# GpSimd adds for the conv LayerNorm sums, half of the first merge moved earlier, and a quartered load, in a hybrid recurrence/convolution block on eight Trainium2 cores

## The chip, the cores and the metric

The kernel runs on the eight cores of one Trainium2 chip, one batch row of 4096 tokens on each core; the cores do not talk to each other. The metric is the device time of one execution, taken on the slowest core, in microseconds (us). Cores 0 to 3 are die 0, cores 4 to 7 are die 1.

Some executions, of every kernel here, fall into a slower state: one die, at times both, shows a lower granted TensorE clock (0.81 to 0.97, where an undisturbed die shows 0.98 to 0.99) and the time is 1 to 20 per cent longer. Only fast runs are compared. On some chips one die was disturbed in most runs; there I also use the *undisturbed-die mean*: the median of a die's four cores, averaged over all runs, slow ones too, and all dies whose median clock was at least 0.98. It leaves out the slowest core and so is about 12 us shorter than the time, but it is compared only with the same figure of the kernel before on the same chip.

Five engines run in parallel, each in its own strict order: TensorE (PE in the profile), VectorE (DVE), ScalarE (ACT), GpSimd (POOL) and SyncE (SP, which issues most DMA transfers here).

## The reference, cut to what matters

```python
proj = h @ w_in            # q, f, i, o-gate | glu value, glu gate | merge gate A, merge gate B
# mixer A: HGRN2 gated recurrence (chunks of 64), then rms_norm, gate, and
y_a = o @ w_hg_out
# mixer B: GLU -> causal depthwise conv of 31 taps -> LayerNorm -> silu -> pointwise
u   = glu_v * sigmoid(glu_g)
u   = causal_depthwise_conv(u, conv_w, conv_b)
u   = silu(layer_norm(u, conv_ln_g, conv_ln_b))     # "conv LN": mean and variance over 1024 channels
y_b = u @ w_conv_out
mixed = sigmoid(gate_a) * y_a + sigmoid(gate_b) * y_b            # "merge"
h = layer_norm(alpha * h + mixed @ w_out)                        # "outproj"
h = layer_norm(alpha * h + (silu(g) * u_) @ w_ffn_out)           # "ffn1", "ffn2"
```

Shapes: 4096 tokens a core, width 1024, feed-forward width 2816.

## The kernel before

The program is recorded first and then list-scheduled: every operation gets an engine, a modelled duration and a place in that engine's queue, and the place is fixed when the kernel is built. What an engine finds at its head and cannot start yet blocks all that stands behind it (one such wait of 8.0 us is followed through the trace below).

**Phase 1** has 32 steps (4 head pairs, 8 tiles of 512 tokens) of the recurrence. A step is a chain: it needs TensorE, then ScalarE, VectorE and GpSimd, then TensorE again. The gaps of that chain are filled with 144 units of GLU and convolution work. A conv unit is 32 small matmuls into one PSUM bank, a copy into one of two store buffers, and a DMA store of the conv output to DRAM (`ys`). `CLEAD` says how many steps before the end the conv units must all be recorded.

```python
yst = [A.at(f"y{i}", yo + i * 2048, [128, 4, 128], F32) for i in range(2)]     # two store buffers
...
def conv_unit(q, g):
    ...
    mmg(lst, ...)                                   # conv matmuls into PSUM bank ps
    ys = yst[G % 2]
    for r0, n in rows:                              # copy PSUM -> store buffer, on ACT or DVE
        cp_any(ys[r0:r0 + n, :, ::-1], ps[r0:r0 + n].rearrange("p (a b) -> p a b", a=4), scale=0.5)
    for jj, (r0, n) in enumerate(rows):             # store buffer -> DRAM
        dma("sp", dst, ys[r0:r0 + n], ..., wr=[("ys", G, jj)], nbytes=600000)
    relps("c", ps)
```

**Phase 2** goes over eight tiles: conv LN (`conv_ln`), merge (256 matmuls, eight weight blocks of 1 MB), outproj (64), transposes of h (`h_trans`), ffn1 (352) and ffn2 (176). In conv LN, TensorE adds over the channels by multiplying with a matrix of ones, 16 matmuls a tile:

```python
def conv_ln(pool="a"):
    pS1, pS2 = newps(pool), newps(pool)
    for j in range(8):                              # 8 blocks of 128 channels
        ts_(b1[:], cpre[:, j, :], cb[:, j:j + 1], None, ALU.add, ALU.bypass)     # DVE: y + bias, to bf16
        act(b2[:], cpre[:, j, :], AF.Square, bias=cb[:, j:j + 1])                # ACT: its square
        mmg([(pS1, ones1024[:], b1[:], j == 0, j == 7)])
        mmg([(pS2, ones1024[:], b2[:], j == 0, j == 7)])
        yield
    ...                                             # mean, 1/std, then 8 x (DVE, DVE, ACT) -> un
```

The **transition** from phase 1 to phase 2 is a queue of work recorded behind the last conv unit:

```python
def tail():
    load_cpre(0)                                    # 2 MB of conv output, needs the last conv store
    loads(0)
    yield from conv_ln("c")
    load_cpre(1)
    yield from merge(0, ...)
```

Steady state of phase 2, tile i: outproj(i) and ffn2(i-1), `h_trans(i)`, merge(i+1), then ffn1(i) with conv LN of tile i+2 spread under it.

## Time and profile before

Time before: 2432.92 us, median of three runs (2431.75 to 2434.59).

The page of the profiled execution, kernel before, first its line of busy time (us, share of the span, instructions), then the shares of the chain of waits that ended last:

```profile
PE 2321.6 (96%) x14400; PEld 1145.9 (47%) x14400; DVE 1349.1 (56%) x1917; ACT 1002.6 (41%) x1391; POOL 114.2 (5%) x287
...
PE 90%; DMA 3%; DVE 2%; ACT 2%; issue 2%; SPq 0%; POOL 0%; DVEq 0%; ACTq 0%; POOLq 0%
```

TensorE is the bound. So a change can win only where it takes work from TensorE or removes time in which TensorE waits or runs below full clock. The windows of the slowest core (core 5) say where such time lies. Columns: stretch in us, its length, busy time and instructions of each engine, granted TensorE clock, DMA share and GB/s.

```profile
core 5: us, PE busy (x) PEld busy (x) DVE busy (x) ACT busy (x) POOL busy (x), PEclk, DMA share, GB/s
60.00:740.00 680.00, 671.43 (x5928) 378.29 (x5925) 503.73 (x686) 449.16 (x574) 92.70 (x233) 0.99 0.80 137
740.00:860.00 120.00, 98.84 (x1142) 59.61 (x1142) 74.67 (x116) 77.86 (x93) 13.85 (x34) 0.95 0.82 208
860.00:945.00 85.00, 69.75 (x319) 30.99 (x316) 40.19 (x66) 29.99 (x43) 0.59 (x1) 0.88 0.51 164
945.00:1025.00 80.00, 76.98 (x375) 34.97 (x376) 57.41 (x90) 38.78 (x58) 0.53 (x1) 1.00 0.66 229
```

Phase 1 up to 740 us leaves TensorE idle for 9 us of 680. From 740 to 1025 us it is idle for 39 of 285 us, and its clock falls. The largest waits of TensorE (for what, us in total, times, longest), first of 60 to 740 us, then of 740 to 1025 us:

```profile
PE pst L442 <- DVE sb_y_18_60 L497: 5.9, 1, 5.9
```
```profile
PE pst L442 <- ACT sb_q_64_106 L469: 11.6, 2, 10.6
PE pst L454 <- DVE sb_K_28_70 L478: 7.7, 2, 4.8
```

The largest gap ends at 885.42 us: after its first eight matmuls merge 0 waits until conv LN 0 has given back scratch tiles. The timeline shows it, and that the eight matmuls after the gap took 3.57 us, where eight of the same shape take 1.89 us in the steady part:

```profile
885.42 3.57 PE L442 MATMUL pst<-sb_xT_55,sb_W_8_50 128*128 128x512 bf16 x8 [10.57 <-ACT sb_q_64_106 L469]
```

For the rest of the text I use three marks on the TensorE timeline, means over cores 0, 1, 2, 3 and 5: **conv** (the last conv unit starts), **mix** (the first outproj matmul of tile 0), **H0** (the first h-transposes of tile 0). Before: conv at 826.0, mix at 934.7, H0 at 1008.3 us; after H0 a tile takes 191.1 us.

### The profile page before, as it was taken

Reading aid. Unit: us, or ns where it says so; the run is one execution under the profiler, and the core shown is the slowest. Engines: PE = TensorE matmul, PEld = TensorE weight load, DVE = VectorE, ACT = ScalarE, POOL = GpSimd, SP = SyncE. Lnnn points to the kernel's source line nnn. Section 1 sums busy time; section 2 is a strip of 40 time slices with the busy share of each in tenths; the row PEclk is TensorE's granted clock in tenths of the full one; section 3 lists DMA queues with packets and bytes.
Section 4 is the critical chain, followed back from the end, with each engine's and each line's share of the span. In section 5 each row is a group of like instructions: output and inputs, shape, how many; then the busy total and the mean of one; then the engine's idle time right before and its main releaser. Section 6 shows DMA issues by size and latency. Waiting matters only on the chain.

```text
span 2430.7 us, 39791 instructions; the slowest of 8 cores (2415.1 to 2430.7 us)
## 1 busy us (share of the span) xinstructions
PE 2321.6 (96%) x14400; PEld 1145.9 (47%) x14400; DVE 1349.1 (56%) x1917; ACT 1002.6 (41%) x1391; POOL 114.2 (5%) x287
## 2 busy tenths in 40 slices
PE   5999999999998869999999999999999999999997
PEld 2555545555555534444444444444444444444443
DVE  1877767777775665546445545534634724721724
ACT  4657756766665653332242242232223323311220
POOL 0211111111110100000000000000000000000000
PEclk8999999999999989999999999999999999999999
DMA  8577996799788855653663654654654663453441
GB/s 228 82 101 113 159 148 139 142 156 149 148 150 190 223 177 202 223 186 126 235 219 136 225 191 144 244 175 169 222 189 153 207 211 146 161 213 144 147 181 70
DMA packets 115824, 414.60 MB, mean 171 GB/s; under 512 B 9248, under 2 KB 42144, under 8 KB 87456
## 3 DMA queue, kind: packets, MB, share of 16 engines
q1 hardware_dynamic: 99760, 360.31, 45.0%
q0 software_dynamic: 15872, 51.74, 16.3%
q8 instruction: 119, 1.95, 0.3%
q14 instruction: 73, 0.60, 0.1%
HBM read 421.81 MB, written 70.58 MB: 203 GB/s over the span
## 4 chain that ended last, share of the span: by engine, by line
PE 90%; DMA 3%; DVE 2%; ACT 2%; issue 2%; SPq 0%; POOL 0%; DVEq 0%; ACTq 0%; POOLq 0%
PE pst L442 89%; DMA ys<-sb_y_18_60 1%; DMA sb_stg_20_62<-xt 1%; PE pst L454 1%; DMA sb_stg_20_62<-w 1%; SPq L523 0%; ACT sb_hb_69_111 L504 0%; DVE sb_R_65_107 L478 0%; ACT L469 0%; ACT sb_F_26_68 L469 0%; ACT sb_F_27_69 L469 0%; DVE sb_q_63_105 L487 0%; ACT sb_hT_93 L499 0%; ACT sb_osq_78 L469 0%; ACT sb_og_32_74 L469 0%
## 5 line engine op out<-in xcount | busy, mean ns | idle before, releaser
L469 ACT ACT_TABLE_LOAD x136 | 174.5, 1283 | 128.9 <-DVE sb_st_74_116 L926 104.8
L442 PE MATMUL pst<-sb_W_12_54,sb_xT_55 128*128 128x512 bf16 (+1 forms) x768 | 152.7, 348 | 20.0 <-ACT sb_xT_55 L568 19.8
L442 PE MATMUL pst<-sb_xT_55,sb_W_8_50 128*128 128x512 bf16 x576 | 134.3, 387 | 16.3 <-ACT sb_q_64_106 L469 10.6
L442 PE MATMUL pst<-sb_W_9_51,sb_xT_55 128*128 128x256 bf16 (+1 forms) x768 | 120.3, 308 | 3.2 <-ACT sb_og_32_74 L469 2.0
L442 PE MATMUL pst<-sb_xT_55,sb_W_10_52 128*128 128x512 bf16 x512 | 115.3, 379 | 2.0 <-DVE sb_v_75 L495 1.0
L442 PE MATMUL pst<-sb_hT_93,sb_W_12_54 128*128 128x512 bf16 x512 | 113.4, 379 | 1.4 <-DVE sb_st_77_119 L924 1.4
L442 PE MATMUL pst<-sb_hT_93,sb_W_67_109 128*128 128x512 bf16 x512 | 114.1, 379 | 0.0
L442 PE MATMUL pst<-sb_hT_93,sb_W_10_52 128*128 128x512 bf16 x512 | 113.6, 379 | 0.0
L442 PEld LDWEIGHTS pst<-sb_W_12_54,sb_xT_55 128*128 128x128 bf16 x768 | 73.9, 98 | 79.6 <-issue 25.1
L442 PE MATMUL pst<-sb_hT_93,sb_W_8_50 128*128 128x512 bf16 x480 | 106.9, 379 | 0.2 <-ACT sb_hT_93 L499 0.2
L442 PE MATMUL pst<-sb_W_11_53,sb_xT_55 128*128 128x512 bf16 (+1 forms) x512 | 92.1, 330 | 6.2 <-DVE sb_y_18_60 L497 5.9
L442 PEld LDWEIGHTS pst<-sb_xT_55,sb_W_8_50 128*128 128x128 bf16 x576 | 56.5, 99 | 87.2 <-issue 23.4
L442 PE MATMUL pst<-sb_hT_93,sb_W_66_108 128*128 128x512 bf16 x416 | 92.4, 379 | 0.0
L442 PEld LDWEIGHTS pst<-sb_W_9_51,sb_xT_55 128*128 128x128 bf16 x768 | 73.8, 98 | 37.8 <-issue 4.3
L442 PE MATMUL pst<-sb_hT_93,sb_W_9_51 128*128 128x512 bf16 x384 | 85.3, 379 | 0.0
L478 DVE TENSOR_TENSOR sb_R_50_92<-sb_R_50_92,sb_lnt_90 128x1024 f32<-128x1024 f32 x64 | 78.4, 1225 | 7.0 <-DVE sb_R_50_92 L478 0.5
L478 DVE TENSOR_TENSOR sb_R_65_107<-sb_R_65_107,sb_lnt_90 128x1024 f32<-128x1024 f32 x64 | 78.4, 1225 | 6.7
L787 DVE TENSOR_TENSOR_SCAN sb_F_26_68<-sb_smask_49,sb_F_26_68 128x512 f32<-128x512 f32 x64 | 74.8, 1208 | 9.7 <-ACT sb_F_26_68 L469 9.6
L469 ACT ACTIVATE sb_q_63_105<-pst 128x512 f32<-128x512 f32 x53 | 31.6, 597 | 117.3 <-PE pst L442 117.2
L469 ACT ACTIVATE sb_q_64_106<-pst 128x512 f32<-128x512 f32 x54 | 32.2, 597 | 114.5 <-PE pst L442 114.2
L442 PEld LDWEIGHTS pst<-sb_hT_93,sb_W_12_54 128*128 128x128 bf16 x512 | 50.0, 98 | 61.7 <-issue 1.5
L442 PEld LDWEIGHTS pst<-sb_hT_93,sb_W_10_52 128*128 128x128 bf16 x512 | 50.1, 98 | 60.4
(283 smaller groups left out, 4293.5 us busy)
## 6 DMA issues: line engine op xcount, KB each, us to landing
sb_W_8_50<-w2b SPq DMA_DIRECT2D x34, 1024.0 KB, 5.8
sb_W_12_54<-w2b SPq DMA_DIRECT2D x34, 1024.0 KB, 6.3
sb_W_9_51<-w2b SPq DMA_DIRECT2D x34, 1024.0 KB, 5.4
sb_W_66_108<-w2b SPq DMA_DIRECT2D x34, 1024.0 KB, 5.4
sb_W_10_52<-w2b SPq DMA_DIRECT2D x32, 1024.0 KB, 6.0
sb_W_67_109<-w2b SPq DMA_DIRECT2D x32, 1024.0 KB, 6.2
w2b<-w POOLq DMA_DIRECT2D x54, 512.0 KB, 13.2
sb_T_16_58<-tabb SPq DMA_DIRECT2D x32, 632.0 KB, 9.5
```

The source lines that it names most:

```text
L442: i = e.matmul(o, lhsT=l, rhs=r, start=s0, stop=s1)
L454: i = e.transpose(o, i_, ident)
L469: P.add("act", lambda e: e.activation(out=out, in_=in_, func=func, **kw), ks(in_, scale, bias) + list(er), (ks(out) if wkeys is None else ...
L478: P.add(eng, lambda e: e.tensor_tensor(out=out, in0=in0, in1=in1, op=op), ks(in0, in1), ks(out) if wkeys is None else wkeys, dur=d)
L787: P.add("dve", lambda e, f2r=f2r: e.tensor_tensor_scan(out=f2r, data0=smask[:], data1=f2r, initial=0.0, op0=ALU.mult, op1=ALU.add), ks(F2[ ...
```

## The change

Three intents. (1) GpSimd, 5% busy, adds the eight channel blocks (and the eight blocks of squares), so that two statistic matmuls a tile are left instead of 16. (2) The conv output of tile 0 is loaded in quarters, and the conv is finished earlier (`CLEAD` 4), so that conv LN 0 starts earlier. (The loads of the later tiles become four DMAs too.) (3) Merge 0 is split around it: the half that needs no conv output (gate A, 128 matmuls) is recorded in the last four recurrence steps, the other half after conv LN 0; the eight weight blocks are loaded twice. `TBIAS`, which is added to the place of the transition's work in the scheduler's list, goes to 0.

```diff
-CLEAD = 2
+CLEAD = 4
-TBIAS = 200
+TBIAS = 0
@@ once: the sum of all bias values, per partition @@
+for a, b in ((20, 4), (44, 2), (44, 1)):
+    tt_(pp[:, 44:44 + b], pp[:, a:a + b], pp[:, a + b:a + 2 * b], ALU.add)
@@ the first GLU blocks: PSUM of the conv pool in place of the recurrence pool (cut) @@
@@ load_cpre @@
-    dma("sp", cpre[:], src, "cpre", rd=[the stores of all 64 conv units], nbytes=1750000)
+    for q in qs:                       # quarters of 512 KB, each waits for its own conv stores
+        dma("sp", cpre[:, 2 * q:2 * q + 2, :], src, f"cp{q}", rd=[stores of quarter q], nbytes=440000)
@@ conv_ln @@
-    for j in range(8):
-        ts_(b1[:], cpre[:, j, :], cb[:, j:j + 1], None, ALU.add, ALU.bypass)
-        act(b2[:], cpre[:, j, :], AF.Square, bias=cb[:, j:j + 1])
-        mmg([(pS1, ones1024[:], b1[:], j == 0, j == 7)])
-        mmg([(pS2, ones1024[:], b2[:], j == 0, j == 7)])
-        yield
+    for j in range(8):
+        act(sq[:], cpre[:, j, :], AF.Square, bias=cb[:, j:j + 1])
+        if j:
+            tt_(S1[:], cpre[:, 0, :] if j == 1 else S1[:], cpre[:, j, :], ALU.add, eng="pool")
+            tt_(S2[:], prev[:] if j == 1 else S2[:], sq[:], ALU.add, eng="pool")
+        yield
+    ts_(b1[:], S1[:], pp[:, 44:45], None, ALU.add, ALU.bypass)
+    cp(b2[:], S2[:])
+    mmg([(pS1, ones1024[:], b1[:], True, True)])
+    mmg([(pS2, ones1024[:], b2[:], True, True)])
@@ tail (shortened) @@
-    load_cpre(0); loads(0); conv_ln("c"); load_cpre(1); merge(0, ...)
+def tail_a(): loads(0); merge(0, "c", (0,))               # gate A half, from step 28 on
+def tail_b(): load_cpre(0, range(3)); (when the conv is done) load_cpre(0, (3,)); conv_ln(0); load_cpre(1)
+run(merge(0, "a", (1,)))                                  # gate B half, after both
```

## The prediction

> **What bounds it now.** TensorE. The page gives PE 96% of the 2430.7 us span, and 89% of the chain of waits is its matmul line. By windows (slowest core):
> - 60 to 740 us (phase 1): PE idle about 9 us in all.
> - 740 to 1025 us (end of phase 1, tile 0, tile 1): PE busy 245.6 of 285 us, so about 39 us idle. The granted clock falls to 0.67-0.94 in four of the windows, about 11 us more. The largest single gap is 10.6 us at 885 us: the first merge waits until conv LN of tile 0 is done; conv LN itself waits for the last conv stores and a 2 MB load of conv output (issued 846, first used 861 us).
> - after 1025 us: a steady 191.1 us per tile, with PE busy 188.4.
>
> **Removed.** 14 of 16 statistic matmuls per tile, 112 in all. A dense matmul of 512 columns costs 0.2158 us (776 in 167.49 us in the chain), so 3.02 us a tile, 24 us together. Tiles 2 to 7 sit in the full-PE regime: 6 x 3.02 = 18 us, directly on the critical path. The 6 us of tiles 0 and 1 fall in the transition.
>
> **Added.** 14 fp32 adds of 128x512 a tile on GpSimd. The trace before has no such add (its POOL TENSOR_TENSORs have 8 columns). The Trainium skill, "GPSIMD Engine Reference", section 3.1, gives 4497 ns for 2048 columns; scaled, my estimate is 1.1-1.3 us each, 15-20 us a tile. The built order puts the two statistic matmuls after nine of 22 ffn1 steps (9 x 3.45 = 31 us), and the eight adds of the first sum can run earlier, so I expect no PE wait in steady state. The same page says that GpSimd shares its SBUF interface with VectorE instructions that have two SBUF inputs; VectorE is only half busy, so some stretching is harmless. Also added: 8 MB more weight loads, since merge 0 reads each block twice.
>
> **Moved.** Conv work ends two steps earlier (PE already full: neutral). Half of merge 0 (128 matmuls, 27.6 us) fills the last four recurrence steps; each holds some 17 us of its own PE work in a chain of 22-24 us. Conv LN 0 runs under them.
>
> **Transition.** Full-speed work there is 245.6 - 11 - 6 = 229 us. I expect some 24 us left over: 2-3 us a step from PE's fixed order; GpSimd's queue, where adds for tiles 0 and 1 stand ahead of the last step's small copies; and DMA, because 5-8 MB of weights plus LN tables, x and output-projection weights are wanted in about 40 us (at most 300 GB/s was seen). So about 253 us, not 285: gain 32. Startup stays DMA-bound: no gain.
>
> **Time.** 2433 - 18 - 33 = 2382 us; 8 in 10 between 2362 and 2404. Faster by over 2%: 0.54; within 2%: 0.44; slower: 0.02.
>
> **Signs.** Right: the tile period falls from 191.1 to about 188.1 us; PE count 14288; GpSimd adds near 1.2 us with PE never waiting for them in phase 2; the 10.6 us gap gone; PE idle between 740 us and the end of merge 1 near 20 us. Wrong: PE waiting on the converted sums (tiles b), i.e. adds over 2 us; PE waiting on weight tiles or the tile-1 x load; E/r copies late behind adds, so K transposes wait.
>
> **What would break it.** Adds much slower than estimated under VectorE contention; DMA starvation in merge 0's second half eating the gain; conv stores slowed in phase 1; or, the other way, a nearly gapless transition (2362).

## The result, and the profile after

Time after: 2424.23 us, median of four runs (2425.72, 2422.74, 2421.01 fast, 2783.92 slow; 2422.74 is the median of the fast ones); before, in the same rounds, 2433.76 us, median of four (2431.75 to 2437.04). The ratio is 0.9955, with an interval of 0.9936 to 0.9975. Ratios here are the mean time of one kernel's fast runs over that of the other's of the same rounds, so not quite the ratio of the medians that I quote. In the same setting a second time (run e11) it was 0.9944. So the kernel is about 11 us faster, where I had predicted 51 us.

The page of the profiled execution, kernel after, the same two lines:

```profile
PE 2301.2 (95%) x14288; PEld 1134.4 (47%) x14288; DVE 1338.9 (55%) x1880; ACT 1009.2 (42%) x1399; POOL 260.9 (11%) x399
...
PE 80%; DVE 7%; DMA 6%; issue 3%; ACT 2%; POOL 0%; SPq 0%; DVEq 0%; ACTq 0%; POOLq 0%
```

112 matmuls are gone and TensorE is busy 20 us less, but the span fell by 6.5 us in this pair of executions: TensorE's part of the chain of waits fell from 90 to 80%, and VectorE and DMA took its place. The windows of core 5, kernel after, same columns as before:

```profile
core 5: us, PE busy (x) PEld busy (x) DVE busy (x) ACT busy (x) POOL busy (x), PEclk, DMA share, GB/s
60.00:740.00 680.00, 654.58 (x5749) 364.57 (x5748) 489.52 (x669) 441.43 (x559) 83.01 (x226) 0.99 0.80 138
740.00:860.00 120.00, 109.52 (x1230) 65.72 (x1229) 79.77 (x119) 86.29 (x107) 30.91 (x46) 0.99 0.71 185
860.00:945.00 85.00, 70.58 (x390) 34.91 (x389) 51.87 (x77) 44.99 (x58) 22.59 (x19) 0.93 0.80 263
945.00:1025.00 80.00, 73.20 (x344) 32.84 (x342) 55.53 (x79) 31.15 (x50) 19.28 (x15) 0.99 0.72 236
```

The first row is the surprise: between 60 and 740 us, where the change was to do nothing, TensorE now idles for 25 us instead of 9 and has issued 179 matmuls fewer. The gain of 740 to 860 us (11 us more busy) is in part work that was left over. The waits of TensorE, kernel after, core 5, first of 60 to 740 us, then of 740 to 1025 us:

```profile
PE pst L447 <- DVE sb_u_15_57 L492: 10.1, 5, 8.0
PE pst L447 <- DVE sb_v_75 L500: 5.8, 2, 4.4
```
```profile
PE pst L447 <- ACT sb_part_94 L474: 6.7, 2, 4.9
PE pst L447 <- DMA sb_W_12_54<-w2b: 6.5, 2, 4.5
PE pst L447 <- DVE sb_U_41_83 L492: 2.2, 1, 2.2
PE pst L447 <- DVE sb_mixed_101 L483: 1.9, 1, 1.9
```

The 10.6 us gap is gone, as predicted; a row of shorter ones has come, on the first half of merge 0 (`part`), on weight blocks (`W <- w2b`), on the recurrence (`U`) and on the merge result. The longest wait of phase 1, 8.0 us on `sb_u`, is a GLU output that comes late. The chain of waits of core 5 tells why (start in us, duration in us, what):

```profile
315.97 0.61 ACT sb_y_19_61 L504
...
316.64 30.16 DMA ys<-sb_y_19_61
...
346.97 0.06 DVE sb_y_19_61 L502
...
347.58 1.25 DVE sb_u_15_57 L492
...
348.96 16.10 PE pst L447 x126
```

Read it from the top: ScalarE fills a store buffer; its store to DRAM takes 30.16 us (a 256 KB store lands in a median of 8.0 us here); VectorE, in its fixed order, has a conv copy into that same buffer at its head and waits for the store; behind it stands the GLU write `sb_u`, for which TensorE waits. Such a wait is not new: on the same core of the kernel before, a store at the same place (313 to 346 us) took 33.55 us, and TensorE waited 5.9 us behind it (`sb_y` above). The example shows how the wait comes about; the change made this one 2 us longer, and added others, as of 4.4 us at 555 us. I followed all engines from 60 us to H0 on five cores:

| mean of cores 0, 1, 2, 3, 5, us | before | after |
|---|---|---|
| TensorE idle, 60 to 740 | 6.7 | 20.5 |
| TensorE idle, 740 to H0 | 35.5 | 30.8 |
| lost to a lower clock, 60 to H0 | 10.1 | 12.3 |
| the rest: TensorE's own work and the shortest gaps | 896.0 | 893.8 |
| H0 | 1008.3 | 1017.4 |
| H0 to the end of TensorE's work | 1402.0 | 1388.7 |

(The rest is H0 less 60 and less the three rows above it. Idle time, here and below, leaves out gaps under some 0.15 us; with every gap counted, the four figures are 7.4, 21.6, 35.6 and 30.7. Clock loss is one less the granted clock, times TensorE's busy time, summed over windows of 20 us.) So the transition, which was to bring 32 us, is 9 us *later*; the part behind it gained 13 of 18 us.

### The profile page after: what moved, and what is told of

The parts are those of the page before. It is cut to its first block, busy times and chain, and to the rows that moved or that the text cites. A ratio compares the mean times of both kernels' runs of the same rounds, so it can differ in the third digit from the quotient of the medians.

```text
span 2424.2 us, 39922 instructions; the slowest of 8 cores (2411.4 to 2424.2 us)
## 1 busy us (share of the span) xinstructions
PE 2301.2 (95%) x14288; PEld 1134.4 (47%) x14288; DVE 1338.9 (55%) x1880; ACT 1009.2 (42%) x1399; POOL 260.9 (11%) x399
## 4 chain that ended last, share of the span: by engine, by line
PE 80%; DVE 7%; DMA 6%; issue 3%; ACT 2%; POOL 0%; SPq 0%; DVEq 0%; ACTq 0%; POOLq 0%
PE pst L447 79%; DMA ys<-sb_y_19_61 2%; DVE sb_R_70_112 L483 2%; DMA sb_stg_20_62<-xt 1%; DVE sb_R_50_92 L483 1%; DMA sb_W_12_54<-w2b 1%; DMA sb_T_16_58<-tabb 1%; PE pst L459 1%; DMA sb_stg_20_62<-w 1%; DVE sb_R_70_112 L488 1%; DVE sb_R_70_112 L492 0%; DVE sb_R_50_92 L492 0%; DVE sb_R_50_92 L488 0%; DVE sb_st_81_123 L946 0%; DVE sb_st_80_122 L946 0%
## 5 line engine op out<-in xcount | busy, mean ns | idle before, releaser
L447 PE MATMUL pst<-sb_xT_55,sb_W_8_50 128*128 128x512 bf16 x560 | 130.4, 385 | 12.3 <-ACT sb_part_94 L474 4.9
L447 PEld LDWEIGHTS pst<-sb_W_12_54,sb_xT_55 128*128 128x128 bf16 x768 | 74.5, 99 | 84.7 <-issue 30.2
L447 PEld LDWEIGHTS pst<-sb_W_9_51,sb_xT_55 128*128 128x128 bf16 x768 | 73.7, 98 | 40.1 <-issue 5.4
L447 PEld LDWEIGHTS pst<-sb_xT_55,sb_W_8_50 128*128 128x128 bf16 x560 | 54.8, 99 | 80.5 <-issue 18.5
L474 ACT ACTIVATE sb_q_68_110<-pst 128x512 f32<-128x512 f32 x51 | 30.4, 597 | 121.1 <-PE pst L447 115.2
L447 PEld LDWEIGHTS pst<-sb_xT_55,sb_W_10_52 128*128 128x128 bf16 x528 | 50.7, 98 | 64.0 <-issue 6.2
L447 PEld LDWEIGHTS pst<-sb_hT_93,sb_W_12_54 128*128 128x128 bf16 x512 | 50.0, 98 | 61.8 <-issue 1.6
L447 PEld LDWEIGHTS pst<-sb_hT_93,sb_W_10_52 128*128 128x128 bf16 x512 | 50.1, 98 | 60.4
```

Of the source, the lines that this page charges most:

```text
L447: i = e.matmul(o, lhsT=l, rhs=r, start=s0, stop=s1)
L474: P.add("act", lambda e: e.activation(out=out, in_=in_, func=func, **kw), ks(in_, scale, bias) + list(er), (ks(out) if wkeys is None else ...
```

## The experiments

Eighteen runs on four chips; all results were correct. The traces of the kernels before and after were taken in earlier rounds; between two chips the same kernel's H0 differs by 2.9 us (after and e11) and 5.6 us (e5 and e12), so smaller differences of H0 between runs of different chips are not read. Theories are named by letters, or in words: **L** (the GpSimd sums help in the steady tiles and hurt in the transition, where VectorE is on the path), **P** (the half of merge 0 came too late because it had to wait for the conv's PSUM banks), and, for phase 1, **W** (conv copies wait for one of the two store buffers) against **D** (conv work crowded earlier puts VectorE and ScalarE work ahead of the recurrence's own, whatever the buffers). In the texts of e1 and e3, D is an earlier theory: that the denser conv work waits for its own DMA, loads of conv taps and conv stores; W is what became of the second half of it.

### One part of the change at a time

**e1, the kernel before with CLEAD 4 alone.**

```diff
-CLEAD = 2
+CLEAD = 4
```

> The kernel before with one constant changed: conv work ends four steps before the end of phase 1 instead of two. Theory D (denser conv work starves on its DMA: tap loads and conv stores): PE idle between 60 and 720 us rises from 9 us to 20 us or more, as in the changed kernel (22 us), and the time is 5 to 20 us longer than before (2438 to 2453). Rival (the phase 1 loss comes from the new PSUM order of the first GLU blocks or from the rest of the new order): PE idle in 60 to 720 us stays at 8 to 11 us and the time within 4 us of before, or shorter since conv LN can start earlier.

Measured (this chip disturbed die 1 in most runs): 2455.57 us median of four fast runs against 2439.41 of three, ratio 1.0038 [0.9971, 1.0106], which decides nothing; undisturbed-die mean 2440.3 against 2426.4, so 14 us slower. On this chip I read the marks on cores 0 to 3 only, the undisturbed die, and give those of before on the same cores in brackets. TensorE's idle time from 60 to 740 us is 15.1 us (6.2), less than the 20 of theory D and more than the 11 of its rival. The conv is *not* over earlier: it starts its last unit at 825.8 us (823.9). H0 is at 1015.1 (1005.6). Asking for the conv earlier only made phase 1 longer.

**e2, the kernel before with the GpSimd sums in all tiles.** The edit is the `conv_ln` part of the diff above.

> The kernel before with only the GpSimd sums (two statistic matmuls a tile); conv pace, tile 0 load and merge 0 as before. If the sums do what the prediction said, the time falls by 18 to 24 us (2409 to 2415) and the tile period is 188.1 us. Rival (GpSimd's adds slow VectorE and PE loses part of it again, as the 188.1 to 189.9 us periods of the changed kernel hint): period 189 us or more, gain 8 to 14 us.

Measured: ratio 1.0016 [0.9883, 1.0149] (unclear); undisturbed-die mean 3 us below before. On cores 0 to 3 it takes 1389.7 us from H0 to the end (1402.8), but between conv and mix TensorE idles 33.9 us (23.7), and H0 comes at 1020.7 (1005.6). First sign that the sums take back in the transition what they bring later.

**e3, the kernel after with CLEAD 2.**

```diff
-CLEAD = 4
+CLEAD = 2
```

> The changed kernel with the conv pace of before (conv work ends two steps before the end). Theory D: phase 1 idle is back at 9 us, and the time is 5 to 15 us shorter than the changed kernel (2409 to 2419), even though half of merge 0 then has fewer steps to fill. Rival: no shorter, or longer, because half of merge 0 and conv LN of tile 0 start later (2424 to 2440).

All its runs were slow ones, so it has no ratio. On the undisturbed die 2421.3, against 2426.4 before: no better than the change as it is, since H0 comes at 1025.2. The half merge and conv LN 0 then stand behind a conv that ends at 862.7 us. But TensorE's idle time from 60 to 740 us is 10.7 us on cores 0 to 3, where the kernel after has 19.3 and the one before 6.2: most of what phase 1 lost goes with `CLEAD`.

**e4, the kernel after with the statistic matmuls back on TensorE** (CLEAD 4, quarters and the split stay).

> The changed kernel with the statistics by 16 matmuls a tile again (for tile 0 in one go, since two PSUM banks cannot be held while merge 0 uses them): only conv pace, quarter loads and the split of merge 0 remain. If the restructure is worth nothing or less on the chip, the time is 2433 to 2450 us (0 to 17 us slower than before); if it gave the 32 us that the prediction wanted, 2401 us. I expect 2438.

Only one fast run (2453.88), so no ratio; undisturbed-die mean 2424.3 against 2426.4, and 1398.9 us from H0 on (1402.8). TensorE's idle time from 740 us to H0, cores 0 to 3, falls to 21.3 us (34.9): without the sums the restructuring does close most of the gap that I had aimed at. But from 60 to 740 us it idles 21.5 us (6.2), and H0 is at 1011.4 (1005.6). What the split gives after 740 us, phase 1 has taken before it.

**e5, the kernel before with the GpSimd sums in tiles 2 to 7 only.**

```diff
 def conv_ln(i):
+    if i < 2:   # the 16 statistic matmuls, as before
+    else:       # GpSimd adds, two matmuls
```

> The kernel before with GpSimd sums for tiles 2 to 7 only; tiles 0 and 1 keep 16 statistic matmuls. Theory L: the sums gain some 12 to 15 us in the steady part (first h transposes to the end) and lose that again in the transition, where their serial adds lengthen conv LN of tiles 0 and 1 (with sums everywhere, conv end to merge 0 took 59 us instead of 53, and start of outproj 0 to the first h transposes 76.5 instead of 73.6). Then this kernel has the transition of before (109 us from the last conv unit to outproj 0, 73.6 us on to the first h transposes) and the steady part of the changed kernel (1387 to 1391 us): 10 to 15 us shorter than before in the same rounds. Rival (the loss comes from schedule noise or GpSimd contention anywhere): the transition is longer than before all the same, and the gain is under 6 us.

Measured: 2422.67 and 2420.79 us in the fast runs, ratio 0.9944 [0.990, 0.9989]; undisturbed-die mean 13 us below before. H0 is at 1007.4, as before; H0 to the end is 1389.5, as in the kernel after. Theory L holds: all that the change gains is here, without its transition. Its gain after H0 is 12.5 us, not 18: five tile periods fall from 191.1 to 188.1 us with a stop of about 1.7 us or more in about every third (the kernel before has such stops too, in five of 25 periods), and the first, under which the sums of tile 2 are made, rises from 116.1 to about 117.8 us.

### The split of merge 0

The build fixes the order on TensorE. From recurrence step 27 on, with K the transposes that each step has, c a conv unit, A one eighth of the first half of merge 0, un the first use of conv LN 0:

```
before  K27 c c c K28 c c c c K29 c c K30 c c c c c K31 K32 un
after   K27 c c K28 c c K29 c c c c K30 c A A A A K31 A A A A un
e1      K27 c c K28 c c c c K29 c c c K30 K31 K32 un
```

All eight parts stand *behind* the last conv unit, which stands where it stood before, between steps 30 and 31. "Fills the last four recurrence steps" was not what the scheduler built.

**e6, the first half in the PSUM tiles of the recurrence**, so that it need not wait for the conv's banks (order: `K28 c A c A c c K29 A c A c K30 A c A K31 A A un`).

```diff
-ps, py = newps(pool), newps(pool)
+ph = newps("h"); ps, py = ph[:, 0:512], ph[:, 512:1024]
...
-yield from merge(0, "c", (0,))
+yield from merge(0, "h", (0,))
```

> The changed kernel, but the first half of merge 0 takes its PSUM from the recurrence's three two-bank tiles instead of the two banks that the conv units use. In TensorE's order its eight parts then stand between the recurrence steps 28 to 31 and between conv units, where in the changed kernel all eight stand behind the last conv unit. Theory P (the shared conv banks pushed the half merge behind the conv work, so it filled nothing): TensorE idle up to the last conv unit falls from 31 to about 20 us, outproj 0 starts 8 to 15 us earlier than in the changed kernel, and so the time. Rival (PSUM of the recurrence is what limits it, or DMA): no gain, or the steps get longer.

Measured: ratio 1.0068 [0.9986, 1.015], undisturbed-die mean 5 us above before; conv at 856.4 and H0 at 1028.2 us (cores 0 to 3, here and in e7 and e8). Now the half does lie in steps 28 to 31, and nothing is gained: the conv ends 18 us later than in the kernel after on the same cores (838.2), and H0 comes later too. Theory P falls. That TensorE had no free time there to fill is my reading; it is not tested by itself.

**e7, e6 with the sums only in tiles 2 to 7.**

> Both together: half merge 0 in the recurrence's PSUM tiles, GpSimd sums for tiles 2 to 7 only, the rest as in the changed kernel. If theories L and P both hold, it beats the kernel before by 20 to 30 us and the changed kernel by 10 to 20 us on the same chip; steady part 1387 to 1391 us, outproj 0 at about 925 us. If only one holds, it is level with e5 or e6.

Ratio 0.9986 [0.9941, 1.0031]; H0 at 1017.3. About 6 us better than e6 on the undisturbed dies (2422.4 against 2428.5), again in favour of L, but no better than before (2423.1).

**e8, the kernel after without the split.**

```diff
-yield from merge(0, "c", (0,))
+yield
...
-run(merge(0, "a", (1,)))
+run(merge(0, "a"))
```

> The changed kernel without the split of merge 0 (one read of its weights, whole merge after conv LN of tile 0; conv pace, quarter loads and sums stay). If the split gains little because its half stood behind the conv work, conv end to outproj 0 grows by less than 8 us against 101.6 us; the 8 MB of extra weight loads are gone. If the split did what the prediction said, it grows by 15 to 27 us.

Ratio 1.0023 [0.999, 1.0056], undisturbed-die mean 6 us above before. Conv to mix takes 114.7 us (after: 101.6), so the split is worth 13 us behind the conv. It works, at half the 27.6 us that its matmuls take.

**e9, e5 with the quarter loads and CLEAD 3**, an attempt at a better kernel.

```diff
-CLEAD = 2
+CLEAD = 3
+for q in qs: dma("sp", cpre[:, 2 * q:2 * q + 2, :], ...)
```

> The kernel before with the GpSimd sums in tiles 2 to 7 only (as e5), plus conv output of tile 0 loaded in quarters and CLEAD=3. If the single 2 MB load of the conv output is what makes conv LN 0 late, the wait of TensorE between the last conv unit and the first outproj-0 matmul falls from 24 us to under 17 and the time falls 5 to 8 us below e5. If asking the conv to be done earlier costs its own filler in phase 1, as e1 showed for CLEAD=4, the idle time of TensorE before the last conv unit rises by 4 us or more and the time stays within 4 us of e5 or is above it.

Ratio 1.0013 [0.9956, 1.0069]; idle before the conv's end 24.7 us and between conv and mix 24.9 us: the first theory fails on both its numbers, the second holds. The quarters, here together with CLEAD 3, did not shorten the wait behind the conv; they were not run alone.

### Do GpSimd adds slow VectorE?

In the kernel after, on core 0, the LayerNorm of outproj 0 looks like this on VectorE (start, us in all, engine, line, operation, count):

```profile
953.78 4.49 DVE L483 TENSOR_TENSOR sb_R_50_92<-sb_R_50_92,sb_lnt_90 128x1024 f32<-128x1024 f32 x2
...
967.40 4.30 DVE L483 TENSOR_TENSOR sb_R_50_92<-sb_R_50_92,sb_lnt_90 128x1024 f32<-128x1024 f32 x2
...
973.49 2.56 DVE L483 TENSOR_TENSOR sb_R_50_92<-sb_R_50_92,sb_lnt_90 128x1024 f32<-128x1024 f32 x2
```

and GpSimd, same kernel and core, in the same time:

```profile
955.90 3.50 POOL L483 TENSOR_TENSOR sb_cmean_106<-sb_cmean_106,sb_cpre_100 128x512 f32<-128x512 f32 x2 [0.92 <-DMA sb_cpre_100<-ys]
965.28 3.14 POOL L483 TENSOR_TENSOR sb_cmean_106<-sb_cmean_106,sb_cpre_100 128x512 f32<-128x512 f32 x2 [5.88 <-DMA sb_cpre_100<-ys]
968.62 4.21 POOL L483 TENSOR_TENSOR sb_cmean_106<-sb_cmean_106,sb_cpre_100 128x512 f32<-128x512 f32 x2 [0.20 <-POOL sb_cmean_106 L483]
```

Two VectorE operations, a row of the view, take 4.3 to 4.5 us while GpSimd adds, and 2.56 us, their time in the kernel before, once it has stopped at 972.8 us. The adds, 1.25 to 1.28 us alone, take up to 2.1 here. The Trainium skill, "SBUF — State Buffer", section "Who interferes with whom", says that a VectorE instruction with two SBUF inputs, or one in a 2-port mode, contends with a GpSimd instruction that reads SBUF, and that the one that comes second waits for the whole of the other. To see it apart from everything else:

**e10, e5 plus twelve GpSimd adds that nobody waits for**, three after each block of outproj 0.

```diff
-    stt(r, r, 2.0 * ALPHA, ps, ALU.mult, ALU.add, wkeys=ks(r) + [("out", i)])
+    stt(r, r, 2.0 * ALPHA, ps, ALU.mult, ALU.add, wkeys=ks(r) + [("out", i), ("dm", i, tb, nb)])
+if i == 0:
+    for k in range(3):
+        P.add("pool", lambda e: e.tensor_tensor(out=smask[:], in0=smask[:], in1=smask[:], op=ALU.add), ...)
```

(`smask` is not used any more at that point, so the output stays right.)

> e5 plus 12 GpSimd adds of 128x512 whose results nobody waits for, three after each block of outproj 0. If GpSimd adds slow VectorE's two-input elementwise work by sharing its way into SBUF, VectorE's 128x1024 adds of that stretch take 1.6 to 2.2 us instead of 1.22, and the stretch from the first outproj-0 matmul to the first h-transpose grows from 73.6 us to 75 or more. If the slowdown in the changed kernel had another cause (order, or the waits on the sums themselves), the VectorE adds stay at 1.22 to 1.3 us and the stretch at 73.6.

Measured: mix to H0 takes 81.1 us, against 74.0 in e5's repeat on the same chip (e12); TensorE's idle time in it is 6.7 against 2.4, and some 2.7 us more go to a lower clock, where e12 loses none; the ratio to before is 0.9948 [0.9898, 0.9998], and the undisturbed-die mean is 2420.8 against 2413.0. VectorE of e10, core 5:

```profile
973.90 1.76 DVE L484 TENSOR_SCALAR sb_R<-sb_R,sb_st 128x1024 f32<-128x1024 f32 x1
975.77 4.30 DVE L479 TENSOR_TENSOR sb_R<-sb_R,sb_lnt 128x1024 f32<-128x1024 f32 x2
...
980.59 1.48 DVE L946 BATCH_NORM_STATS2 sb_st<-sb_R 128x6 f32<-128x512 f32 x2
```

GpSimd of e10, core 5 (`smask` is a dummy add, `cmean` a sum of tile 2):

```profile
967.02 3.67 POOL L968 TENSOR_TENSOR sb_smask<-sb_smask 128x512 f32<-128x512 f32 x3 [0.20 <-POOL sb_smask L968]
...
973.04 5.95 POOL L479 TENSOR_TENSOR sb_cmean<-sb_cmean,sb_cpre 128x512 f32<-128x512 f32 x3
980.81 3.40 POOL L968 TENSOR_TENSOR sb_smask<-sb_smask 128x512 f32<-128x512 f32 x3 [1.82 <-DVE sb_R L488]
```

VectorE of e12 (the same kernel without the twelve adds), core 5, and below it GpSimd:

```profile
963.17 1.48 DVE L945 BATCH_NORM_STATS2 sb_st<-sb_R 128x6 f32<-128x512 f32 x2
...
973.99 0.81 DVE L483 TENSOR_SCALAR sb_R<-sb_R,sb_st 128x1024 f32<-128x1024 f32 x1
974.91 2.55 DVE L478 TENSOR_TENSOR sb_R<-sb_R,sb_lnt 128x1024 f32<-128x1024 f32 x2
```
```profile
958.64 10.19 POOL L478 TENSOR_TENSOR sb_cmean<-sb_cmean,sb_cpre 128x512 f32<-128x512 f32 x6
```

The pair of two-input operations goes from 2.55 to 4.30 us, and the `TENSOR_SCALAR` from 0.81 to 1.76; `BATCH_NORM_STATS2`, with one SBUF input, keeps its 0.74 us each while GpSimd was adding (980.81 to 989.8 us). This case agrees with the page. The slow operations shown did not meet a dummy add: they met sums of tile 2, which the dummy adds had pushed back from 957 to 969 us (e12) to 971 to 990 us. In e12 these sums slow one pair of outproj 0, in e10 dummy adds and sums together slow three. It is shown that twelve adds which nobody waits for cost 7 us here.

**e11, the kernel after again, and e12, e5 again**, on the chip of e9 and e10.

> The changed kernel again, on the chip of e9, e10 and e12: 0.4 to 0.5 per cent below the kernel before in fast runs, 2 to 8 us above e5 (e12) if the sums and CLEAD of its transition cost more than they bring; equal to e12 or below it if e5's better time came from its chip.

> e5 again: 10 to 15 us below the kernel before, and 2 to 8 us below the changed kernel, if the theory that the sums help in the steady tiles and hurt in the transition holds; no better than the changed kernel if e5's figure was luck of the chip.

Fast runs of e11: 2426.66 to 2436.61 us, ratio 0.9944 [0.9907, 0.9981]; of e12: 2422.16 to 2427.74 us, ratio 0.9924 [0.9884, 0.9964]. Undisturbed-die means: before 2431.4, e11 2419.5, e12 2413.0. So e5 beats the kernel before in two settings. Against the kernel after, on the one chip that ran both, the intervals overlap; the undisturbed-die means are 6.5 us apart, as is H0 in the traces (7 us earlier).

### What took the time in phase 1?

The waits of conv copies on a store of conv output (`DMA ys`), VectorE and ScalarE together, 60 to 840 us, mean of five cores, are 6.1 us before, 14.5 after and 15.1 in e11; in e1, mean of four cores, 17.0. They are also 8.6 us in e5 and 11.9 in e12, which keep CLEAD 2 and lose little in phase 1, so this sum is no measure of what TensorE loses. Three lines of waits (for what, us in total, times, longest): VectorE of the kernel before, core 5; VectorE of e1, core 0; ScalarE of e1, core 0.

```profile
DVE sb_y_18_60 L497 <- DMA ys<-sb_y_18_60: 9.0, 1, 9.0
```
```profile
DVE sb_y L497 <- DMA ys<-sb_y: 9.8, 1, 9.8
```
```profile
ACT sb_y L499 <- DMA ys<-sb_y: 12.7, 6, 4.4
```

A wait of VectorE need not cost TensorE anything, so I took the waits away. There was no room for four f32 buffers; in bf16, four fit in the place of two. That also halves the bytes of the store and of the load.

```diff
-ys_d = nc.dram_tensor("ys", [D, S], F32).ap()
+ys_d = nc.dram_tensor("ys", [D, S], BF16).ap()
-yst = [A.at(f"y{i}", yo + i * 2048, [128, 4, 128], F32) for i in range(2)]
+yst = [A.at(f"y{i}", yo + i * 1024, [128, 4, 128], BF16) for i in range(4)]
-ys = yst[G % 2]
+ys = yst[G % 4]
-cpre = inU("cpre", [128, 8, TS], F32)
+cpre = inU("cpre", [128, 8, TS], BF16)
```

**e13, this edit on the kernel before; e14, on e1; e15, on the kernel after; e16, on e5.** All on the chip of e9 to e12.

> The kernel before with its conv output kept in bf16 instead of f32 (half the bytes of store and load) and four store buffers instead of two. If waits of the conv copies for free store buffers cost TensorE time in phase 1, its idle time before the last conv unit falls from 16 us to 12 or less and the time by 3 to 8 us; if not, the time stays within 3 us of before. bf16 input also shortens nothing else on the critical path except the load of conv output.

> e13 plus CLEAD=4, the counterpart of e1. Theory W (conv units crowded by CLEAD=4 wait for store buffers): idle time of TensorE before the last conv unit is 18 us or less where e1 had 25, and the first h-transpose of tile 0 is no later than in e13. Theory D (the crowded units put VectorE and ScalarE work ahead of the recurrence's own, whatever the buffers): idle time stays at 22 us or more, at least 6 above e13, and the h-transpose comes 5 to 10 us later than in e13.

> The changed kernel with bf16 conv output and four store buffers. Theory W: idle time before the last conv unit falls from 31 us to 20 or less, the time 8 to 12 us below the changed kernel. Theory D: it stays at 26 or more and the time falls by under 5 us.

> e5 (GpSimd sums in tiles 2 to 7) with bf16 conv output and four store buffers: the candidate to beat e5. If store waits matter at all, 3 to 8 us below e5, that is 14 to 20 us below the kernel before; if not, the same as e5, 10 to 15 us below before.

The waits on `DMA ys` are gone from VectorE and ScalarE in all four. Means of five cores (e1: four), us, and the undisturbed-die mean less that of before:

| | idle 60 to 740 | idle before conv | H0 | less before | ratio of fast runs |
|---|---|---|---|---|---|
| e13 before + bf16, 4 buffers | 8.9 | 17.7 | 1010.8 | -2.1 | 1.0004 [0.9977, 1.003] |
| e1 CLEAD 4 (cores 0 to 3) | 15.1 | 25.5 | 1015.1 | +13.9 | 1.0038 [0.9971, 1.0106] |
| e14 CLEAD 4 + bf16, 4 buffers | 10.6 | 20.2 | 1004.3 | -3.3 | 1.0007 [0.9914, 1.01] |
| e11 after | 21.2 | 32.2 | 1020.3 | -11.9 | 0.9944 [0.9907, 0.9981] |
| e15 after + bf16, 4 buffers | 14.9 | 22.6 | 999.3 | -24.6 | 0.9936 [0.9838, 1.0034] |
| e12 sums in tiles 2 to 7 | 9.6 | 19.4 | 1013.0 | -18.4 | 0.9924 [0.9884, 0.9964] |
| e16 e12 + bf16, 4 buffers | 9.6 | 18.0 | 1009.9 | -17.2 | 0.9918 [0.9889, 0.9946] |

The kernel before gains nothing from the edit (e13), nor does e5 (e16): at CLEAD 2 the store buffers cost them nothing that shows in the time, and my hope for e13 and e16 was wrong. With CLEAD 4 it is different: e1's H0 was 9.5 us later than before's on the same cores, e14's is 6.5 us *earlier* than e13's, and the idle time that CLEAD 4 adds before the conv's end falls from 10.2 us (25.5 less 15.3 on cores 0 to 3) to 2.5 us (20.2 less 17.7). In undisturbed-die means of one chip each, CLEAD 4 cost 14 us with two buffers (e1 against before) and nothing with four (e14 is 1 us below e13). The order on TensorE from step 27 on is the same in both but for one conv unit, which moved by two steps (`K28 c c c c K29 c c c K30 K31 K32` in e1, `K28 c c c K29 c c c K30 c K31 K32` in e14), but in steps 23 to 25 the conv units lie differently too, so order is not excluded. The traces tell more. I followed each gap of TensorE from 60 to 840 us back through what released it, until TensorE is met again. Gaps whose way leads over a store of conv output make 2.8 of 18.7 idle us before and 10.8 of 28.4 in e1 (cores 0 to 3): 8 of the 10 us that CLEAD 4 adds, but up to 740 us only 2.5 of 8.6. In e13 and e14 there are none, and the idle time is 19.1 and 20.7 us. So theory W holds in part: the waits for stores are there, they grow with CLEAD 4, and with four buffers they and the lost time go. How much of e14's gain is its new order is not shown, so D is not excluded; W's own mark of 18 us or less before the conv's end was missed by e14 with 20.2. The kernel after gains 13 us more from the edit (24.6 less 11.9) and its H0 moves up by 21 us, of which some 13 are idle time and 8 lost clock. Its waits of TensorE from 60 to 740 us on core 5 (e15); where the kernel after had 8.0 us in one wait for `sb_u`, the longest is 0.6:

```profile
PE pst L447 <- DVE sb_u L492: 3.8, 8, 0.6
PE pst L447 <- ACT sb_osq L474: 2.4, 2, 1.4
PE pst L447 <- DMA sb_T<-tabb: 2.3, 1, 2.3
```

W does not explain all of it: I had written 20 us or less of idle time before the conv's end for e15, and it is 22.6, with 14.9 up to 740 us where e13 has 8.9. The same walk through the traces says so too: gaps behind a store are 3.4 us before and 7.9 after (five cores), 4.5 of the 14 us that phase 1 lost up to 740 us. The remaining 6 us of e15 I can only see as short waits on ScalarE, VectorE and a tap load, and leave open. e15's ratio has a wide interval because in one of its three fast runs (2445.51 us) cores 2 and 3 ran at a clock of 0.973 and 0.976, where the other cores had 0.99; the others, 2415.98 and 2410.32, are the two fastest executions.

**e17, e15 with two bf16 buffers; e18, e15 with the statistic matmuls of tiles 0 and 1 back on TensorE.** On a fourth chip.

```diff
-yst = [... for i in range(4)];  ys = yst[G % 4]         # e17
+yst = [... for i in range(2)];  ys = yst[G % 2]
```

> e15 with two store buffers in place of four. If the number of buffers is what helped, TensorE's idle time before the last conv unit is back at 27 us or more (e15 had 18 to 25) and the time is 6 us or more above e15's, that is within 0.5 per cent of the changed kernel's gain over before. If bf16 itself (half the bytes stored and loaded, faster VectorE reads of the conv output) helped, the idle time stays at 25 us or less and the time within 4 us of e15's, 20 us or more below before.

> e15 with the statistic matmuls back on TensorE for tiles 0 and 1, in one go for tile 0: the candidate to beat all. If the sums cost conv LN 0 and tile 1 what e2 and e5 showed (5 to 12 us), it runs 3 to 8 us below e15, 25 to 32 us below before; if four buffers and bf16 have already hidden that cost, it equals e15 within 3 us or is above it.

e17: 2465.79 us median of five fast runs against 2444.23 of seven, ratio 1.007 [1.0012, 1.0128], undisturbed-die mean 2.8 us above before. The copies wait for stores again (9.2 us a core), the idle time before the conv's end is 35.9 us, H0 is at 1028.5. So half-size data alone does not help, which points to the number of buffers. One reserve: the scheduler, which models the buffers too, built another order for two bf16 buffers (five conv units in a row before step 30), and a 10.3 us wait on ScalarE at 820 us belongs to that order, so e17's size is not the buffers' alone. A 128 KB store landed in 7.1 us (e15) to 8.2 us (e18) at the median of core 2's phase 1, no sooner than 256 KB in the kernel after (7.0 and 8.1 for its two buffers, same core): its pieces of 256 bytes are half as long. The Trainium skill, "DMA: Bandwidth & Descriptors", "Specifications", gives 512 bytes as the least for line rate; the landing times fit that, but they also hold the wait behind other traffic, so they do not test it.

e18: two fast runs, 2424.24 and 2422.33 us, ratio 0.9921 [0.9889, 0.9954], undisturbed-die mean 18.9 us below before. I had expected it below e15; it is not. With four buffers, taking the sums off GpSimd in the transition brought nothing that shows (two chips, so no closer than this).

Which version is best? e12, e16 and e18 have ratios of 0.992 (e5, the same kernel as e12, 0.9944), e15 has 0.9936 with the lowest single runs and the lowest die mean. e5, e12, e16 and e18 beat the kernel before; e15's interval includes 1. Against the kernel after (0.9955 and 0.9944) and among each other, the intervals overlap, and I cannot rank them by these runs.

## Why the prediction was wrong, point by point

I predicted 2382 us; the three fast runs after are 2421 to 2426. TensorE as the bound, the durations of undisturbed operations and the mechanism of the steady part were right. The transition's share (32 us in its paragraph, 33 in the sum) was not.

1. **"Conv work ends two steps earlier (PE already full: neutral)" failed, and cost most.** The conv's last unit stayed between steps 30 and 31, and came 13.6 us *later* (839.6 against 826.0). TensorE lost 14 us before 740 us (20.5 against 6.7), a stretch to which I had given no change at all. Shown: CLEAD 4 alone costs 9 us of idle time there (e1), CLEAD 2 gives most of it back (e3), and four half-size store buffers in place of two, with the order that the scheduler builds for them, undo it (e14 against e13) and win 13 us in the kernel after (e15). In the traces 4.5 of the 14 us lie directly behind conv stores; whether the rest is the order or waits further back is open. That TensorE was full had been read from the kernel before, and did not say what the same work needs when it is asked for sooner. "Conv stores slowed in phase 1" stands in my list of what could break the prediction; I had given it no number.
2. **"Half of merge 0 (27.6 us) fills the last four recurrence steps" failed.** All its parts stood behind the last conv unit; the built order, which I had, shows it. The split is worth 13 us behind the conv (e8), and moving it into the steps (e6) gains nothing, so "17 us of its own PE work in a chain of 22-24 us" did not leave time that could be used. That the conv units fill it already is how I read it; e6 shows only that nothing is gained.
3. **"So about 253 us, not 285: gain 32" is the mis-sized sum.** It took 39 us of idle time down to 24, and all 11 us of lost clock to nothing. Measured from 740 us to H0, idle time went from 35.5 to 30.8, and the clock loss there did not change (8.5 and 8.5): one gap of 10.6 us became several of 2 to 5 us. The Trainium skill, "TensorE: Matmul & The Clock Gate", Part 1, describes the clock as set by how busy TensorE was recently; eight matmuls after a gap took 3.57 us where 1.89 is usual. In e15 and e14, with fewer gaps, the loss there is 4.5 and 3.8 us.
4. **"VectorE is only half busy, so some stretching is harmless" failed.** It is half busy over the span, but in outproj 0 and conv LN it is on the chain: e10's idle adds cost 7 us. The same stretching is seen on the adds of tile 2, which in e5, e12 and the kernel after begin under outproj 0; that this is why the first period rises is likely, and not tested by itself.
5. **"6 x 3.02 = 18 us" was of the right kind and one tile too large.** Five tile periods together fell by 15.3 us, 3.0 each; the stops of about 1.7 us, in about every fourth period, are in the kernel before too. The sixth, the first period, in which most sums of tile 2 are made, was to fall by 3 and rose by 1.3 us. From H0 on the kernel gains 13.3 us (e5: 12.5).
6. **Right:** the adds (predicted 1.1 to 1.3 us; 1.25 to 1.28 alone; the mean of all 112 on core 5 is 1.35, the longest 2.25, in contention), the period of 188.1 us, 14288 matmuls, no wait of TensorE on the converted sums after 1025 us, the 10.6 us gap gone, and no gain at startup.

The account on five cores: +14 us (idle before 740) - 5 (idle after it) + 2 (clock) - 2 (work) = +9 at H0, less 13 behind it, gives -4 in this pair of executions; the runs as a whole give -11.

What stays open: how much of the loss in phase 1 is the store buffers' and how much the order's; the last 6 us of idle time in phase 1 of e15; how much of e17's loss is its order; and the stops of 1.7 us, which I see (TensorE waiting for VectorE's LayerNorm statistics and ScalarE's bf16 copy before transposes) but did not test.

## What to carry to other kernels

A filler that is asked for earlier is not free because the engine it runs on looks full: it also needs its buffers back sooner, so count what each unit holds (here a store buffer, for up to 30 us of DMA) before moving it, and test the move alone. Work put on an idle engine is charged to whoever shares memory access with it and stands on the chain in that stretch, so apply it by stage: the sums paid in the steady tiles and, with two store buffers, cost about as much as they brought in the transition (e2). And when a scheduler places the work, read the built order before counting on where a piece will run.

## What the Trainium skill lacked or had wrong

- "GPSIMD Engine Reference", section 3.1: its 4497 ns for an add of 2048 columns, scaled to 512, is 1.12 us (an estimate); the trace has 1.25 to 1.28 us for 512 columns, undisturbed. A measured add of a small size is lacking.
- "SBUF — State Buffer", "Who interferes with whom": the rule holds, but no size for a pair in a steady alternation is given. Here a pair of 128x1024 f32 two-input VectorE operations went from 2.55 to 4.30 us, a 128x1024 `TENSOR_SCALAR` from 0.81 to 1.76, and the 128x512 GpSimd adds from 1.27 to as much as 2.25.
- "DMA: Bandwidth & Descriptors": it does not say how long a small store can take behind other traffic. A 256 KB store landed in a median of 8.0 us, and in up to 30.16 us (33.55 in the kernel before); the 8.0 us wait of TensorE shown above stands behind one of the long ones.
- No page works out what strict queues cost: a stall of one engine on a store buffer can hold back an unrelated write behind it on that queue; one such stall was 5.9 us of TensorE in the kernel before and 8.0 in the kernel after.
